# Recurrent stage: a block's gate products move behind the next block's first projection, and its convolution behind the running block's chain

## The chip, the cores and the metric

One core of one Trainium2 chip. The metric is the device time of one execution in microseconds (us); lower is better. The kernel before: 1864.37 us, median of 3 runs (1861.35 to 1865.53).

## What is computed

One layer of a hybrid decoder over 1024 tokens of width 1024: an input projection, a recurrent branch, an attention branch over selected keys, a merge, and a mixture of experts. The change touches the recurrent branch. Its reference, cut to that:

```python
xr, gr, q, ckv, qi, ki, wi, mg = jnp.split(u @ w_in[l], split_pts, axis=-1)
xc = causal_dwconv(xr, conv_w[l], conv_b[l])               # width 4
r = sigmoid(einsum('bsnc,ncd->bsnd', xc_blocks, w_a) + b_a) # 10 blocks of 128 columns
i = sigmoid(einsum('bsnc,ncd->bsnd', xc_blocks, w_x) + b_x)
log_a = -LRU_C * softplus(-lam) * r
a = exp(log_a)
inp = sqrt(-expm1(2.0 * log_a)) * (i * xc)
h = scan of h[t] = a[t] * h[t-1] + inp[t]
y_a = (gelu(gr) * h) @ w_rnn_out[l]
```

## The kernel before

The kernel runs in stages: head and index, the search for the selected keys beside the projections of queries and merge gates, the recurrent stage (`rnn`), attention, merge, experts. Channels lie on the 128 partitions and tokens along the free axis, so the recurrent branch is ten independent blocks of 128 channels by 1024 tokens. Every product is made of three matmuls of split operands (`mm3`, L137 to L139: high by high, low by high, high by low); `hilo` (L97, L98) splits a tile into a high part on ACT and a low part on DVE.

For each block b the stage does this:

- `project` of the columns of xr, then of gr: per column block, two halves of 512 tokens (`proj_tile`), 24 matmuls each, into a PSUM tile `pj` of a ring of three (`mm`, bufs 3). The weight of a column block is loaded by SP into `raw_in` (ring of 3), split on ACT into `whi_in` (L127) and on DVE or POOL into `wlo_in` (L128), each a ring of 2. `next_in` issues the load and split of the next column block before a block is used. `load_in` puts the low part on POOL for the xr columns of blocks 4 to 7 and for the first xr and gr block, and on DVE for the rest.
- `ev_x` copies xr out of PSUM (L734); with the second half it calls `conv`: an ACT instruction (L741) and three DVE instructions (L745) make `xc`, `hilo` makes `xh` and `xl`, and the two gate weights `gw` are loaded and split into `gh`, `gl`.
- `ev_g` takes the gelu of gr out of PSUM into `ge` (L793, a table load ahead of it); with the second half it calls `block`.
- `block` makes the two gate products (12 matmuls into `pg`, a ring of two PSUM tiles), their sigmoids `tr` and `ti` (L766), then the chain exp (L769), tanh (L770), sqrt (L771) on ACT and on DVE L774 to L785 with the scan L783; the result `ge` goes to `g_spill` (L786).

ACT takes a table load (ACT_TABLE_LOAD) where the next function is in another table. Each engine works through its own queue in order; that order is made at build time by the scheduler of the tile layer from the order in which the code calls, its priorities and the buffers' waits, so an edit of the calling order moves instructions on all engines. After the ten blocks three column blocks of merge gates are projected (`gates_q`, `gq`, L706), and attention begins (`pk`).

Of the kernel before, what the change touches and what calls it, by code (L numbers as in the profile page):

```python
# [19 lines left out]
P = 128  # L20
D = 1024
S = 1024
KT = D // P
ST = S // P
NB = 10
# [42 lines left out]
C_XR, C_GR, C_Q, C_KV, C_QI, C_KI, C_MG, C_END = 0, 1280, 2560, 3584, 3840, 4352, 4424, 6472  # L68
# [13 lines left out]
class Trunk:  # L82
# [638 lines left out]
    def rnn(self):  # L721
        nc, io = self.nc, self.io
        with ExitStack() as st:
            p1 = self.pool(st, "rnn")
            pp = self.pool(st, "rnnps", bufs=2, space=PSUM)
            F = lambda n, b, dt=F32, bufs=1, w=S: p1.tile([P, w], dt, name=f"{n}_{b}", tag=n, bufs=bufs)
            cur = {}

            def ev_x(c, m, ts_, ps):
                b = c // P  # L730
                if ts_.start == 0:
                    cur[b] = F("xr", b, w=S + 3, bufs=2)
                    nc.gpsimd.memset(cur[b][:, 0:3], 0.0)
                nc.scalar.activation(cur[b][:, 3 + ts_.start : 3 + ts_.stop], ps, AF.Copy)  # L734
                if ts_.stop == S:
                    cur[b] = conv(b, cur.pop(b))

            def conv(b, xr):
                c1 = slice(b, b + 1)
                xc, xh, xl = F("xc", b), F("xh", b, F32R), F("xl", b, F32R)  # L740
                nc.scalar.activation(  # L741
                    xc, xr[:, 3 : 3 + S], AF.Identity, scale=self.cw[:, 3 * NB + b : 3 * NB + b + 1], bias=self.cb[:, c1]
                )
                for w in (2, 1, 0):
                    nc.vector.scalar_tensor_tensor(  # L745
                        xc, xr[:, w : w + S], self.cw[:, w * NB + b : w * NB + b + 1], xc,
                        op0=OP.mult, op1=OP.add,
                    )
                self.hilo(xh, xl, xc)
                gh = p1.tile([P, 2, P], F32R, name=f"gh_{b}", tag="gh", bufs=2)  # L750
                gl = p1.tile([P, 2, P], F32R, name=f"gl_{b}", tag="gl", bufs=2)
                gw = p1.tile([P, 2, P], F32, name=f"gw_{b}", tag="gw", bufs=2)
                nc.sync.dma_start(gw[:, 0, :], io["w_rg_a"][0, b])
                nc.sync.dma_start(gw[:, 1, :], io["w_rg_x"][0, b])
                self.hilo(gh, gl, gw)
                return xc, xh, xl, gh, gl

            def block(b, xc, xh, xl, gh, gl):
                c1 = slice(b, b + 1)
                tr, ti = F("tr", b), F("ti", b)  # L760
                for g, (dst, bias) in enumerate(((tr, self.ba), (ti, self.bx))):
                    for h in range(2):
                        s_ = slice(h * 512, (h + 1) * 512)
                        ps = pp.tile([P, 512], F32, name=f"pg_{b}_{g}_{h}", tag="pg")
                        self.mm3(ps, gh[:, g, :], gl[:, g, :], xh[:, s_], xl[:, s_], True, True)
                        nc.scalar.activation(dst[:, s_], ps, AF.Sigmoid, bias=bias[:, c1])  # L766
                sq, w0, w1 = F("sq", b), F("w0", b), F("w1", b)

                nc.scalar.activation(w0, tr, AF.Exp, scale=self.sp8n[:, c1])  # L769
                nc.scalar.activation(tr, tr, AF.Tanh, scale=self.sp4[:, c1])  # L770
                nc.scalar.activation(sq, tr, AF.Sqrt)  # L771
                nc.vector.tensor_tensor(ti, ti, xc, op=OP.mult)

                nc.vector.tensor_scalar(w0, w0, 0.5, 0.5, op0=OP.mult, op1=OP.add)  # L774
                nc.vector.scalar_tensor_tensor(w1, tr, 1.0, w0, op0=OP.add, op1=OP.mult)
                nc.vector.scalar_tensor_tensor(w1, w1, 2.0, w0, op0=OP.subtract, op1=OP.mult)

                nc.vector.scalar_tensor_tensor(sq, sq, -2.0, w1, op0=OP.mult, op1=OP.mult)
                nc.vector.tensor_tensor(ti, ti, sq, op=OP.mult)

                nc.vector.tensor_tensor(tr, tr, w1, op=OP.mult)
                nc.vector.tensor_scalar(tr, tr, 2.0, 1.0, op0=OP.mult, op1=OP.add)
                nc.vector.tensor_tensor_scan(sq, tr, ti, 0.0, op0=OP.mult, op1=OP.add)  # L783
                ge = cur["g"]
                nc.vector.tensor_tensor(ge, ge, sq, op=OP.mult)  # L785
                nc.sync.dma_start(self.gd[b * P : (b + 1) * P, :], ge)  # L786

            def ev_g(c, m, ts_, ps):
                b = (c - C_GR) // P
                if ts_.start == 0:  # L790
                    cur["g"] = F("ge", b, bufs=2)
                ge = cur["g"]
                nc.scalar.activation(ge[:, ts_], ps, AF.Gelu_apprx_tanh)  # L793
                if ts_.stop == S:
                    block(b, *cur.pop(b))

            for b in range(NB):
                self.project(C_XR + b * P, C_XR + (b + 1) * P, ev_x)
                self.project(C_GR + b * P, C_GR + (b + 1) * P, ev_g)


    def attention(self):
# [910 lines left out]
```

## Time and profile before

| what | value |
|---|---|
| runs | 1864.37 us median, 1861.35 to 1865.53 |
| profiled execution, its own time | 1865.06 us |
| its span | 1863.3 us |
| busy: PE, DVE, ACT, POOL | 94%, 77%, 63%, 21% of the span |
| recurrent stage | 402 to 694 us of the span, with the first two of the three `gq` column blocks |

The span begins with the first and ends with the last recorded instruction; 1.8 us lie around it. PE is TensorE's matmuls, PEld its weight loads, DVE VectorE, ACT ScalarE, POOL GpSimd, SP the queue that issues the loads. In a timeline each row has the start and the duration in us, the engine, the line, the operation, out<-in with shapes, and in brackets the idle time ahead of it with what ended that.

### The profile page before, as it was taken

The numbers are of one execution on the slowest core, as the hardware profiler recorded it, in microseconds if no ns is written. First come the engines' busy times: TensorE is split into PE (matmuls) and PEld (weight loads), VectorE is DVE, ScalarE is ACT, GpSimd is POOL, SyncE is SP. The second block draws the span as 40 slices with busy tenths as digits, with TensorE's granted clock in tenths as the row PEclk, the third lists the DMA queues.
The fourth block names the chain that finished last, engine by engine and source line by source line (L and its number), as shares of the span: only waits on it lengthen the run. The fifth ranks groups of instructions, "written<-read, shape, count | busy, mean of one in ns | idle before, by whom it ended". The sixth has DMA issues, their size and how long they took to land. (4 is left out here: it accounts for less than half of the span.)

```text
span 1863.3 us, 24597 instructions
## 1 busy us (share of the span) xinstructions
PE 1759.3 (94%) x8532; PEld 1456.1 (78%) x8532; DVE 1439.9 (77%) x2393; ACT 1170.1 (63%) x1730; POOL 398.8 (21%) x249
## 2 busy tenths in 40 slices
PE   3999999997999999999999999979999999999995
PEld 2788877786777888999788877858888888788774
DVE  6688876697777766778524456569999999999998
ACT  6565677725676767888512113348888887777765
POOL 4101002210010001212000001033554544344134
PEclk9999999998999999999999999979999999999998
DMA  9213754322112212121738544369989999999994
GB/s 297 61 35 104 237 179 147 109 89 65 59 54 73 68 58 93 55 66 57 216 107 252 194 152 170 138 238 350 379 329 344 363 376 367 366 380 371 357 338 182
DMA packets 163738, 366.85 MB, mean 197 GB/s; under 512 B 17855, under 2 KB 107543, under 8 KB 139160
## 3 DMA queue, kind: packets, MB, share of 16 engines
q1 hardware_dynamic: 152112, 340.50, 51.3%
q0 software_dynamic: 10192, 19.99, 3.9%
q10 hardware_dynamic: 1304, 4.74, 0.6%
q8 instruction: 68, 1.11, 0.3%
q14 instruction: 62, 0.51, 0.1%
HBM read 326.90 MB, written 54.53 MB: 205 GB/s over the span
## 5 line engine op out<-in xcount | busy, mean ns | idle before, releaser
L1472 ACT ACTIVATE whi<-raw_w 128x1024 fp32r<-128x1024 f32 x384 | 395.6, 1057 | 107.8 <-DMA raw_w<-in_moe_w_dram 28.2
L1474 DVE TENSOR_TENSOR wlo<-raw_w,whi 128x1024 fp32r<-128x1024 f32 x382 | 447.9, 1220 | 13.1 <-ACT whi L1472 4.7
L139 PE MATMUL pj<-uhi,wlo_in 128*128 128x512 f32 (+2 forms) x784 | 302.8, 387 | 5.6 <-POOL wlo_in L128 4.2
L137 PE MATMUL pj<-uhi,whi_in 128*128 128x512 f32 (+2 forms) x784 | 304.3, 388 | 1.2 <-ACT gq L706 1.2
L138 PE MATMUL pj<-ulo,whi_in 128*128 128x512 f32 (+2 forms) x784 | 302.0, 385 | 0.0
L1543 POOL DMA_INDIRECT h_spill<-ye,idx x30 | 179.4, 5980 | 215.0 <-DVE ye L1539 202.2
L139 PEld LDWEIGHTS pj<-uhi,wlo_in 128*128 128x128 f32 (+1 forms) x784 | 146.4, 187 | 37.8 <-POOL wlo_in L128 6.4
L137 PEld LDWEIGHTS pj<-uhi,whi_in 128*128 128x128 f32 (+1 forms) x784 | 146.6, 187 | 32.1 <-ACT gq L706 2.4
L138 PEld LDWEIGHTS pj<-ulo,whi_in 128*128 128x128 f32 (+1 forms) x784 | 146.6, 187 | 29.9 <-issue 1.0
L654 ACT ACTIVATE junk_a<-B,nt 128x768 bf16<-128x768 f32 (+2 forms) x93 | 96.8, 1041 | 49.6 <-DVE nt L650 41.2
L1501 PE MATMUL pa<-whi,xh 128*128 128x512 f32 x256 | 103.3, 403 | 0.6 <-ACT xh L97 0.5
L138 PE MATMUL py<-wlo,hh 128*128 128x512 f32 x256 | 100.9, 394 | 2.7 <-DVE wlo L1474 2.7
L1501 PE MATMUL pa<-whi,xl 128*128 128x512 f32 x256 | 100.6, 393 | 0.5 <-DVE xl L98 0.5
L137 PE MATMUL py<-gh,whi_y 128*128 128x512 f32 x256 | 99.9, 395 | 1.1 <-ACT gh L97 1.1
L1501 PE MATMUL pb<-whi,xh 128*128 128x512 f32 x256 | 100.0, 391 | 0.4 <-ACTq L1618 0.4
L139 PE MATMUL py<-gh,wlo_y 128*128 128x512 f32 x256 | 100.4, 393 | 0.0
L138 PE MATMUL py<-gl,whi_y 128*128 128x512 f32 x256 | 100.2, 393 | 0.1
L139 PE MATMUL py<-whi,hl 128*128 128x512 f32 x256 | 100.0, 391 | 0.0
L137 PE MATMUL py<-whi,hh 128*128 128x512 f32 x256 | 99.8, 400 | 0.1
L1501 PE MATMUL pb<-whi,xl 128*128 128x512 f32 x256 | 99.7, 389 | 0.0
L128 POOL TENSOR_TENSOR wlo_in<-raw_in,whi_in 128x1024 fp32r<-128x1024 f32 (+1 forms) x20 | 50.3, 2515 | 230.4 <-ACT whi_in L127 230.4
L127 ACT ACTIVATE whi_y<-raw_y 128x1024 fp32r<-128x1024 f32 x16 | 17.0, 1062 | 104.5 <-PE py L138 98.6
(403 smaller groups left out, 4119.2 us busy)
## 6 DMA issues: line engine op xcount, KB each, us to landing
raw_w<-in_moe_w_dram SPq DMA_DIRECT2D x191, 1024.0 KB, 12.6
raw_in<-in_w_in_dram SPq DMA_DIRECT2D x50, 512.0 KB, 3.5
wm<-in_w_mod_dram SPq DMA_DIRECT2D x32, 512.0 KB, 4.7
sg_spill<-gq SPq DMA_DIRECT2D x16, 512.0 KB, 2.6
sg<-sg_spill SPq DMA_DIRECT2D x32, 256.0 KB, 3.2
wm<-in_w_mod_dram SPq DMA_DIRECT2D x24, 256.0 KB, 5.8
g_spill<-ge SPq DMA_DIRECT2D x10, 512.0 KB, 2.6
gr<-g_spill SPq DMA_DIRECT2D x10, 512.0 KB, 3.6
```

The lines of the kernel that those rows point to most:

```text
L127: nc.scalar.activation(hi[:, :n], raw[:, :n], AF.Copy)
L128: eng.tensor_tensor(lo[:, :n], raw[:, :n], hi[:, :n].bitcast(F32), op=OP.subtract)
L137: mm(ps, ah, bh, start=start, stop=False)
L138: mm(ps, ah, bl, start=False, stop=False)
L139: mm(ps, al, bh, start=False, stop=stop)
L654: nc.scalar.activation(junk_a[:, :n], self.B[j], AF.Sign, bias=nt[:, i : i + 1], accum_out=cnt[:, i : i + 1])
L1472: self.last_hi = nc.scalar.activation(hi, part, AF.Copy).ins
L1474: eng.tensor_tensor(lo, part, hi.bitcast(F32), op=OP.subtract)
L1501: nc.tensor.matmul(ps, a[:, kk, :], b[:, k * DE : (k + 1) * DE], start=kk == 0 and a is xh and b is hi, stop=kk == KT - 1 and b is lo,)
L1543: nc.gpsimd.indirect_dma_start(out=self.hd, out_offset=bass.IndirectOffsetOnAxis(ap=idx, axis=0), in_=ye, in_offset=None, bounds_check=S - ...
```

## The change

`conv` and `block` are no longer called from the evacuations. The loop runs once more than there are blocks: in turn b it projects xr of block b, then issues the gate products and the chain of block b-1, then the convolution of block b, then the projection of gr of block b.

```diff
@@ -732,8 +732,6 @@
                     cur[b] = F("xr", b, w=S + 3, bufs=2)
                     nc.gpsimd.memset(cur[b][:, 0:3], 0.0)
                 nc.scalar.activation(cur[b][:, 3 + ts_.start : 3 + ts_.stop], ps, AF.Copy)
-                if ts_.stop == S:
-                    cur[b] = conv(b, cur.pop(b))
 
             def conv(b, xr):
                 c1 = slice(b, b + 1)
@@ -791,12 +789,16 @@
                     cur["g"] = F("ge", b, bufs=2)
                 ge = cur["g"]
                 nc.scalar.activation(ge[:, ts_], ps, AF.Gelu_apprx_tanh)
-                if ts_.stop == S:
-                    block(b, *cur.pop(b))
-
-            for b in range(NB):
-                self.project(C_XR + b * P, C_XR + (b + 1) * P, ev_x)
-                self.project(C_GR + b * P, C_GR + (b + 1) * P, ev_g)
+
+
+            for b in range(NB + 1):
+                if b < NB:
+                    self.project(C_XR + b * P, C_XR + (b + 1) * P, ev_x)
+                if b:
+                    block(b - 1, *parts)
+                if b < NB:
+                    parts = conv(b, cur.pop(b))
+                    self.project(C_GR + b * P, C_GR + (b + 1) * P, ev_g)
```

In the rows of the built order below, `pj_512_0` is the projection of column 512 for tokens 0 to 511: columns 0 to 1279 are xr (512 is block 4, 640 block 5), 1280 to 2559 gr (1664 is block 3, 1792 block 4). `pg_3` is a gate product of block 3; a number at the end of a name is the buffer's. In the changed file the lines behind `ev_x` stand two lower (L766 is L764, L793 is L791).

PE, around the first gate products of block 3, before:

```order
L137 MATMUL pj_512_0_4111<-uhi_0_94,whi_in512_4008 128x512
L138 MATMUL pj_512_0_4111<-ulo_0_102,whi_in512_4008 128x512
L137 MATMUL pg_3_0_0_4068<-xh_3_3992,gh_3_4000 128x512
L137 MATMUL pg_3_0_1_4073<-xh_3_3992,gh_3_4000 128x512
L139 MATMUL pj_512_0_4111<-uhi_0_94,wlo_in512_4009 128x512
L137 MATMUL pj_512_0_4111<-uhi_1_95,whi_in512_4008 128x512
L138 MATMUL pj_512_0_4111<-ulo_1_103,whi_in512_4008 128x512
L138 MATMUL pg_3_0_0_4068<-xl_3_3993,gh_3_4000 128x512
```

The same place of the changed kernel:

```order
L137 MATMUL pj_1792_0_4187<-uhi_0_94,whi_in1792_4067 128x512
L138 MATMUL pj_1792_0_4187<-ulo_0_102,whi_in1792_4067 128x512
L137 MATMUL pj_1792_512_4214<-uhi_0_94,whi_in1792_4067 128x512
L138 MATMUL pj_1792_512_4214<-ulo_0_102,whi_in1792_4067 128x512
L137 MATMUL pj_640_0_4246<-uhi_0_94,whi_in640_4182 128x512
L138 MATMUL pj_640_0_4246<-ulo_0_102,whi_in640_4182 128x512
L139 MATMUL pj_640_0_4246<-uhi_0_94,wlo_in640_4183 128x512
L137 MATMUL pg_3_0_0_4128<-xh_3_3992,gh_3_4000 128x512
L137 MATMUL pg_3_0_1_4133<-xh_3_3992,gh_3_4000 128x512
L139 MATMUL pj_1792_0_4187<-uhi_0_94,wlo_in1792_4068 128x512
```

The gates of block 3 stood behind gr of block 3; they now stand behind the whole of xr of block 4, two matmuls each of both halves of gr of block 4, and three of xr of block 5, the third of which reads a low part made on POOL. Behind the last row shown follow four more matmuls of `pj_1792_0`, then the gate products that read `xl_3`.

ACT, from the tanh of block 2 to the first convolution step of block 3, before:

```order
L770 ACTIVATE tr_2_3892<-tr_2_3892,sp4_1493 128x1024
L734 ACTIVATE xr_3_3962<-pj_384_0_3937 128x512
L771 ACT_TABLE_LOAD
L771 ACTIVATE sq_2_3914<-tr_2_3892 128x1024
L127 ACTIVATE whi_in512_4008<-raw_in512_4007 128x1024
L734 ACTIVATE xr_3_3962<-pj_384_512_3965 128x512
L97 ACTIVATE gh_4_4174<-gw_4_4176 128x256
L741 ACTIVATE xc_3_3991<-xr_3_3962,cols_85 128x1024
```

The same of the changed kernel:

```order
L768 ACTIVATE tr_2_3952<-tr_2_3952,sp4_1493 128x1024
L791 ACT_TABLE_LOAD
L791 ACTIVATE ge_3_4038<-pj_1664_0_4013 128x512
L769 ACT_TABLE_LOAD
L769 ACTIVATE sq_2_3974<-tr_2_3952 128x1024
L739 ACTIVATE xc_3_3991<-xr_3_3923,cols_85 128x1024
L791 ACT_TABLE_LOAD
```

Between tanh and sqrt there is now a gelu with a table load of its own in place of a copy; the other half of that gelu needs another load behind the convolution step.

ACT, from there to the sigmoid of block 3, before:

```order
L793 ACT_TABLE_LOAD
L793 ACTIVATE ge_3_4038<-pj_1664_0_4013 128x512
L97 ACTIVATE xh_3_3992<-xc_3_3991 128x1024
L793 ACTIVATE ge_3_4038<-pj_1664_512_4040 128x512
L127 ACTIVATE whi_in1792_4106<-raw_in1792_4105 128x1024
L766 ACT_TABLE_LOAD
L766 ACTIVATE tr_3_4066<-pg_3_0_0_4068,cols_85 128x512
```

The same of the changed kernel:

```order
L791 ACTIVATE ge_3_4038<-pj_1664_512_4040 128x512
L127 ACTIVATE whi_in1792_4067<-raw_in1792_4066 128x1024
L734 ACTIVATE xr_4_4097<-pj_512_0_4072 128x512
L97 ACTIVATE gh_4_4174<-gw_4_4176 128x256
L127 ACTIVATE whi_in640_4182<-raw_in640_4181 128x1024
L734 ACTIVATE xr_4_4097<-pj_512_512_4100 128x512
L97 ACTIVATE xh_3_3992<-xc_3_3991 128x1024
L764 ACT_TABLE_LOAD
L764 ACTIVATE tr_3_4126<-pg_3_0_0_4128,cols_85 128x512
```

The gelu and the weight split that stood between `xh` and the sigmoid stand ahead of `xh` now, with the copies of xr of the next block and one weight split more; the split `whi_in640` writes the buffer that the second half of `pj_512` reads to its end.

## Rows read from the trace of the kernel before

**Rows 1.** The page, busy time by engine over the span.

```profile
PE 1759.3 (94%) x8532; PEld 1456.1 (78%) x8532; DVE 1439.9 (77%) x2393; ACT 1170.1 (63%) x1730; POOL 398.8 (21%) x249
```

**Rows 2.** Windows, block 0's gates: length, busy PE, PEld, DVE, ACT, POOL, granted clock, DMA share, GB/s.

```profile
430.00:460.00 30.00, 26.33 (x108) 21.19 (x108) 20.66 (x18) 19.96 (x22) 0.20 (x2) 0.88 0.16 51
```

**Rows 3.** Waits, 398 to 682 us: total us, times, longest us.

```profile
ACT xh L97 <- DVE xc L745: 54.0, 9, 12.4
...
PE pg L137 <- ACT xh L97: 17.6, 5, 8.8
```

**Rows 4.** Timeline of PE, the first gate matmuls of blocks 0 to 3 and their neighbours.

```profile
424.06 0.39 PE L139 MATMUL pj<-uhi,wlo_in 128*128 128x512 f32 x1
433.21 0.80 PE L137 MATMUL pg<-xh,gh 128*128 128x512 f32 x1 [8.75 <-ACT xh L97]
...
436.77 0.52 PE L137 MATMUL pj<-uhi,whi_in 128*128 128x512 f32 x1
...
460.25 0.73 PE L137 MATMUL pg<-xh,gh 128*128 128x512 f32 x2
...
485.49 0.73 PE L137 MATMUL pg<-xh,gh 128*128 128x512 f32 x2
...
487.22 0.39 PE L138 MATMUL pg<-xl,gh 128*128 128x512 f32 x1
...
512.78 0.73 PE L137 MATMUL pg<-xh,gh 128*128 128x512 f32 x2 [1.98 <-ACT xh L97]
```

**Rows 5.** Timeline of ACT, from `xh` of block 1 to `xh` of block 2.

```profile
459.13 1.06 ACT L97 ACTIVATE xh<-xc 128x1024 fp32r<-128x1024 f32 x1 [3.70 <-DVE xc L745]
...
461.64 1.28 ACT L766 ACT_TABLE_LOAD   x1
462.94 1.27 ACT L766 ACTIVATE tr<-pg,cols 128x512 f32<-128x512 f32 x2
...
470.18 0.59 ACT L734 ACTIVATE xr<-pj 128x512 f32<-128x512 f32 x1
470.79 1.28 ACT L771 ACT_TABLE_LOAD   x1
472.08 1.06 ACT L771 ACTIVATE sq<-tr 128x1024 f32<-128x1024 f32 x1
...
484.38 1.06 ACT L97 ACTIVATE xh<-xc 128x1024 fp32r<-128x1024 f32 x1 [3.70 <-DVE xc L745]
```

**Rows 6.** Timeline of DVE, blocks 0 and 2.

```profile
427.01 1.22 DVE L128 TENSOR_TENSOR wlo_in<-raw_in,whi_in 128x1024 fp32r<-128x1024 f32 x1
...
484.26 1.22 DVE L128 TENSOR_TENSOR wlo_in<-raw_in,whi_in 128x1024 fp32r<-128x1024 f32 x1
...
485.73 1.22 DVE L98 TENSOR_TENSOR xl<-xc,xh 128x1024 fp32r<-128x1024 f32 x1
```

**Rows 7.** Timelines of POOL and DVE where both work.

```profile
391.05 2.39 POOL L128 TENSOR_TENSOR wlo_in<-raw_in,whi_in 128x1024 fp32r<-128x1024 f32 x1 [8.49 <-ACT whi_in L127]
...
527.42 2.91 POOL L128 TENSOR_TENSOR wlo_in<-raw_in,whi_in 128x1024 fp32r<-128x1024 f32 x1 [15.54 <-ACT whi_in L127]
...
526.86 1.22 DVE L781 TENSOR_TENSOR tr<-tr,w 128x1024 f32<-128x1024 f32 x1
527.99 3.42 DVE L779 TENSOR_TENSOR ti<-ti,sq 128x1024 f32<-128x1024 f32 x1
```

**Rows 8.** Timelines of ACT and PE, the end of the stage.

```profile
593.53 1.06 ACT L97 ACTIVATE xh<-xc 128x1024 fp32r<-128x1024 f32 x1 [6.46 <-DVE xc L745]
...
669.57 1.04 ACT L97 ACTIVATE xh<-xc 128x1024 fp32r<-128x1024 f32 x1
...
673.29 1.27 ACT L766 ACTIVATE tr<-pg,cols 128x512 f32<-128x512 f32 x2 [0.89 <-PE pg L139]
...
672.86 0.40 PE L139 MATMUL pg<-xh,gl 128*128 128x512 f32 x1
...
693.78 0.39 PE L137 MATMUL pj<-uhi,whi_in 128*128 128x512 f32 x1
```

## The prediction

> **What bounds the kernel now.** I read the page first, then a window, the waits and the timelines of the recurrent stage. PE is busy for 94% of the span [rows 1], so over the whole kernel the order of PE's work decides, and PE's idle stretches are what a reordering can give back. In the recurrent stage the window of block 0's gates shows PE busy for 26.33 of 30 us at a mean granted clock of 0.88 [rows 2]. The waits name the cause: PE stood 17.6 us, in five stretches, for `xh`, and ACT's `xh` stood 54.0 us for DVE's `xc` [rows 3]. The longest stretch is block 0: PE ends gr at 424.06 and starts the gates at 433.21, 8.75 us idle [rows 4]; there DVE was still at the search. That is the most that the edit can fill in one place.
>
> The stage has a second limit, and the timelines show it. A block is 96 projection and 12 gate matmuls. From 424.06 back they start 0.2265 us apart (46 of them in 10.42 us), so PE alone needs 24.5 us a block. But the gates of blocks 1, 2 and 3 start at 460.25, 485.49 and 512.78 [rows 4]: 25.2 and 27.3 us apart. The reader should see in ACT's rows that this is a closed loop. From `xh` at 459.13 ACT has no gap until the sqrt ends at 473.14 (14.0 us), and from there DVE needs until `xh` at 484.38 (11.2 us) [rows 5]: chain of block b, then `xc` of block b+1, then its `xh`. 14.0 + 11.2 = 25.2, the period. The blocks with a weight split on POOL have 2.1 us more: POOL's split takes 2.39 us alone, 2.91 us where it begins behind a running DVE instruction, and DVE's next, which takes 1.22 us otherwise, then takes 3.42 [rows 7].
>
> **The change, step by step.** I walk the loop in the new order with the durations of these rows. No arithmetic is added; one table load per block is, and nine of them stand in the loop.
>
> *Block 0.* PE goes on from gr 0 into xr 1, but the third matmul of that needs a low part that DVE makes at 427.01 to 428.23 [rows 6], so about 3.5 of the 8.75 us stay idle. The other 46 matmuls take 10.4 us: 438.7. After the 8.75 us of idling the clock was at its lower level, and the six matmuls from 433.21 to 436.77 took 3.6 us for 1.4 [rows 4], part of it a wait for `xl`; after 1.98 us [rows 4] the projections kept their pace. For 3.5 us I take 0.9, under half of that loss (bounds 0 and 2.2): the gates start at 439.6. ACT first splits the weight of xr 2, whose buffer xr 1 reads to its end, copies the half of xr 1 (0.6), and loads the sigmoid table (1.29): the first sigmoid at 442.4.
>
> *From sigmoid to sqrt.* The stretch from the first sigmoid to the end of tanh stays as it is, 462.94 to 470.18, 7.24 us. Then a table load (1.29) and the gelu (0.61, the price of the copy that stood there) come ahead of the sqrt's load and the sqrt (2.35) [rows 5]: 11.5 us, 1.3 more than before. With DVE's 11.2, `xh` of block 1 starts at 442.4 + 22.7 = 465.1, 6.0 us later than at 459.13.
>
> *Block 1.* Between `xh` and sigmoid ACT has a copy, a split and a load, as now: 3.8 us [rows 5]. `xh` of block 2 starts at 465.1 + 3.8 + 22.7 = 491.6, against 484.38.
>
> *Ordinary blocks.* Copy and split have moved ahead of `xh`, so ACT could begin the sigmoid 2.3 us after `xh`. It can't, since the gate product is not there: `xl` starts 1.35 us after `xh` [rows 6], the first matmul on it 2.84 us after `xh` (487.22), and the sigmoid begins 0.43 us after the start of the next matmul (672.86 to 673.29) [rows 8]: 2.84 + 0.23 + 0.43 = 3.5 us. The period is 3.5 + 11.5 + 11.2 = 26.2 us, where it was 25.2. PE's 24.5 us lie under it.
>
> *Blocks 2 to 5* need a low part from POOL for the third of the matmuls that now stand ahead of their gates. Its split on ACT has to wait until PE has ended the projection that still reads that buffer, some 25 us after the `xh` before, so that POOL starts while DVE is at the last step of `xc`. DVE's next instruction is the low part of gr, then the small `gl`, then `xl`: they wait for POOL's 2.4 us. The gates' second matmul comes at 5.0 instead of 2.84 us after `xh`, the sigmoid at 5.7. Period 5.7 + 22.7 = 28.4, where it was 27.3. I looked for cover and found none: DVE is on the loop throughout.
>
> *Sum to block 9.* 491.6 + 4 x 28.4 = 605.2 for `xh` of block 6 (593.53 before) and + 3 x 26.2 = 683.8 for block 9 (669.57 before) [rows 8]: 14.2 us behind.
>
> *The end.* Before, PE had 101 matmuls between the gates of block 9 and the third merge column, which it began at 693.78 [rows 8]. Now the xr and gr work lies ahead, and after 34 matmuls PE stands before a projection whose PSUM buffer is freed by the first `gq`, which ACT does behind the whole chain of block 9. `xh` to sigmoid is 4.3 us there (11 matmuls between the two gate parts), then 7.24, 2.35, a load 1.29 and `gq` 0.60: 15.8 us, so PE resumes at 699.6 and after 24 matmuls (5.4) begins the third column at 705.0. That is 11.2 us behind. PE's idling of some 6 us before it may put its first matmuls at the lower clock: 0 to 2.2, I take 0.9. From that column on PE's order is unchanged and PE bound, so the delay stays.
>
> Sum: +12.1 us against the profiled 1865.06, 1877.2; that execution was 0.7 above the median of 1864.37. I forecast 1877.
>
> *The added load, weighed.* Each table load of the stage takes 1.28 us, and what follows starts at once (461.64 to 462.94) [rows 5]; 1.29 is in the sum. The Trainium skill, ScalarE: Activation LUTs, What ACT_TABLE_LOAD costs, adds a drain of about 1.38 us to every switch, 2.66 in all, and advises grouping calls by table, which speaks against this order. By it nine loads would cost 12 us more and the sum would be 1890; no row here has that gap.
>
> **Rivals.**
> - *POOL's split falls clear of the loop.* If POOL's split fell where DVE is idle, as it waits for the sigmoids, blocks 2 to 5 would go at 26.2: 8.8 us less, +3.3, some 1868, no difference that counts (0.2%, 3.7 us, is about what a measurement of this kernel can tell from no change). For it: POOL's start hangs on PE's end within half a microsecond. Against: DVE waits wherever POOL meets a two-input instruction [rows 7], and the loop leaves it no gap.
> - *The projection ahead covers the loop: faster.* If gates and chain were no longer the limit, PE would run from 439.6 through its 1032 matmuls to the third column: 439.6 + 233.7 = 673.3, 20 us sooner, 1844. It turns on the period: under 25.5 us on average the change gains, and at 24.5 it gains all of this. For it: the 8.75 us of block 0 do get filled, and PE has a whole projection between `xc` and the gates. Against: the loop runs through ACT and DVE, and it becomes longer by a load, not shorter.
> - *The clock falls in every POOL block.* PE idles there some 4 us in 7. If the lower clock follows, the end of xr moves by up to 2.2 us; ACT's split (1.05) and copy (0.6) of it now stand ahead of `xh` and have 0.3 us to spare, so up to 1.9 reach the loop. With half of that in four blocks and the upper bounds at start and end (2 x 1.3): + 6.4, some 1883. For it: block 0 [rows 2, 4]. Against: after 1.98 us in block 3 PE kept its pace.
> - *A table load costs twice its row*: 9 x 1.28, + 11.5, some 1888.
>
> **How the numbers follow.** Forecast 0.70, POOL clear 0.10, faster 0.05, clock 0.14, dear load 0.01. Faster is 0.05, same 0.10 and slower 0.85 (0.70 + 0.14 + 0.01). The range has to take in POOL's 8.8 us downwards and the clock upwards: 1867 to 1885, which leaves out the faster case, the dear load and the ends of the others.
>
> **What would show it.** Right: the 8.75 us before the gates of block 0 split into some 3.5 us of PE waiting for the low part of xr 1 and no wait at the gates; `xh` of block 1 some 6 us later; `xh` 28.4 us apart from block 2 to 6 and 26.2 after; PE waiting for POOL's low part and for `xl` in blocks 2 to 5; one long PE wait of about 6 us for the first `gq`; six table loads per block. Wrong: periods under 25.5, no PE wait at the end, or `xl` straight behind `xh` in blocks 2 to 5.

## Result, and the profile after

| | before | after |
|---|---|---|
| median of four runs each | 1864.95 us (1861.35 to 1867.93) | 1894.61 us (1890.99 to 1897.13) |
| ratio, 95% interval | | 1.0158 (1.0134 to 1.0183) |
| profiled execution, its own time | 1865.06 us | 1897.13 us |
| its span | 1863.3 us | 1895.4 us |

The change costs 29.7 us; 12.1 were forecast, and 1894.6 lies outside the range. The direction was right, the size was not. The two profiled spans differ by 32.1 us, 2.4 of which arise before the stage: gr of block 0 ends at 426.45 where it ended at 424.06 [rows 4]. (POOL's first split of the stage begins at 401.92 us before and 404.31 after; in the kernels below, whose heads are the same, between 399.87 and 406.19.) Below, 2.39 us are taken off where a time of after stands beside one of before.

The busy line of the page of after [rows 1]: PE is busy 16.0 us longer with as many matmuls, ACT 12.7 us (nine more instructions, the added table loads, are 9 x 1.28 = 11.5 of it), POOL 17.6 us with as many instructions; DVE is not.

```profile
PE 1775.3 (94%) x8532; PEld 1466.4 (77%) x8532; DVE 1430.5 (75%) x2393; ACT 1182.8 (62%) x1739; POOL 416.4 (22%) x249
```

The `xh` rows of ACT and some sigmoids (`tr`), after; the prediction walked from one `xh` to the next.

```profile
434.49 1.06 ACT L97 ACTIVATE xh<-xc 128x1024 fp32r<-128x1024 f32 x1 [12.46 <-DVE xc L743]
...
445.32 1.28 ACT L764 ACT_TABLE_LOAD   x1
446.61 1.26 ACT L764 ACTIVATE tr<-pg,cols 128x512 f32<-128x512 f32 x2
...
469.32 1.06 ACT L97 ACTIVATE xh<-xc 128x1024 fp32r<-128x1024 f32 x1 [5.33 <-DVE xc L743]
...
495.84 1.06 ACT L97 ACTIVATE xh<-xc 128x1024 fp32r<-128x1024 f32 x1
...
527.55 1.06 ACT L97 ACTIVATE xh<-xc 128x1024 fp32r<-128x1024 f32 x1 [0.41 <-DVE xc L743]
...
537.04 0.69 ACT L764 ACTIVATE tr<-pg,cols 128x512 f32<-128x512 f32 x1 [7.14 <-PE pg L139]
...
560.02 1.06 ACT L97 ACTIVATE xh<-xc 128x1024 fp32r<-128x1024 f32 x1
...
623.65 1.06 ACT L97 ACTIVATE xh<-xc 128x1024 fp32r<-128x1024 f32 x1 [0.41 <-DVE xc L743]
...
627.14 1.26 ACT L764 ACTIVATE tr<-pg,cols 128x512 f32<-128x512 f32 x2 [1.13 <-PE pg L139]
...
702.23 1.06 ACT L97 ACTIVATE xh<-xc 128x1024 fp32r<-128x1024 f32 x1 [0.74 <-DVE xc L743]
```

Set beside the walk (before's times from [rows 5, 8]), what was missed lies mostly in one place, blocks 2 to 5, and smaller parts in block 0 and at the end:

| stretch | forecast, us | measured, us |
|---|---|---|
| `xh` of block 1, against before | +6.0 | +7.8 |
| from there to `xh` of block 2 (25.25 before) | +1.2 | +1.3 |
| blocks 2 to 5, `xh` 495.84 to 623.65 (109.15 before) | +4.5 | +18.7 |
| blocks 6 to 8, to 702.23 (76.04 before) | +2.6 | +2.5 |
| `xh` of block 9 to the third merge column (24.21 before) | -2.1 | -0.5 |
| sum, of the unrounded values | +12.1 | +29.8 |

An ordinary period was forecast at 26.2 and is 26.2 (78.58 / 3). A period with a split on POOL was forecast at 28.4 and is 32.0 (127.81 / 4). 14.2 of the missing 17.6 us lie there. Block 3 shows what stands in such a period; first the timelines of POOL and DVE.

```profile
526.73 5.59 POOL L128 TENSOR_TENSOR wlo_in<-raw_in,whi_in 128x1024 fp32r<-128x1024 f32 x1 [26.09 <-ACT whi_in L127]
...
526.24 1.28 DVE L743 SCALAR_TENSOR_TENSOR xc<-xr,cols,xc 128x1024 f32<-128x1024 f32 x1
527.43 1.22 DVE L128 TENSOR_TENSOR wlo_in<-raw_in,whi_in 128x1024 fp32r<-128x1024 f32 x1
528.57 0.42 DVE L98 TENSOR_TENSOR gl<-gw,gh 128x256 fp32r<-128x256 f32 x1
528.90 1.22 DVE L98 TENSOR_TENSOR xl<-xc,xh 128x1024 fp32r<-128x1024 f32 x1
```

And PE in the same stretch, with the first gate matmul of block 6 for comparison:

```profile
526.25 0.39 PE L138 MATMUL pj<-ulo,whi_in 128*128 128x512 f32 x1
...
532.37 0.79 PE L139 MATMUL pj<-uhi,wlo_in 128*128 128x512 f32 x1 [4.45 <-POOL xr L733]
532.96 1.05 PE L137 MATMUL pg<-xh,gh 128*128 128x512 f32 x2
533.82 0.63 PE L139 MATMUL pj<-uhi,wlo_in 128*128 128x512 f32 x1
534.24 0.63 PE L137 MATMUL pj<-uhi,whi_in 128*128 128x512 f32 x1
...
624.76 0.73 PE L137 MATMUL pg<-xh,gh 128*128 128x512 f32 x2 [0.74 <-ACT xh L97]
```

I had POOL take 2.4 us and DVE wait for it. It is the other way round: DVE's low part of gr, `gl` and `xl` run at their usual lengths, `xl` 1.35 us behind `xh` as in an ordinary block, and POOL's split ends at 532.32, 2.20 us behind the end of `xl`. All four are alike: 5.24, 5.59, 5.13 and 5.56 us, each ending 4.77 us behind `xh`. PE stands before the third xr matmul meanwhile. (The row names POOL's tiny memset of `xr`, which begins as the split ends.) Then a second cost follows: matmuls start 0.43 us apart where they stood 0.2265 apart, PE's lower level. A window of 8 us from 532 (columns as in [rows 2]) shows the granted clock at 0.60; one from 718, behind the wait for the first `gq`, at 0.70.

```profile
532.00:540.00 8.00, 7.63 (x21) 6.04 (x22) 0.00 (x0) 2.76 (x4) 0.36 (x2) 0.60 0.54 150
...
718.00:726.00 8.00, 7.70 (x25) 6.15 (x26) 6.31 (x5) 1.23 (x3) 0.00 (x0) 0.70 0.10 40
```

The first sigmoid comes 4.08 us behind the first gate matmul there; in block 6, at full clock, 2.38 (624.76 to 627.14). Over the four blocks that excess is 5.7 us (1.42, 1.70, 1.63, 0.99); the other 8.5 of the 14.2 I put down to POOL's lateness; no run separates the two, since the one follows from the other. PE's waits from 400 to 722 us, all of them (total us, times, longest us):

```profile
PE pj L139 <- POOL xr L733: 17.0, 4, 4.5
PE pj L137 <- ACT gq L706: 6.9, 1, 6.9
PE pg L137 <- ACT xh L97: 4.9, 5, 2.3
PE pj L137 <- ACT xr L734: 3.7, 7, 0.6
PE pj L139 <- DVE wlo_in L128: 3.4, 1, 3.4
```

### The profile page after: what moved, and what is told of

The parts are those of the page before. It is cut to its first block, busy times and chain, and to the rows that moved or that the text cites. A ratio compares the mean times of both kernels' runs of the same rounds, so it can differ in the third digit from the quotient of the medians.

```text
span 1895.4 us, 24592 instructions
## 1 busy us (share of the span) xinstructions
PE 1775.3 (94%) x8532; PEld 1466.4 (77%) x8532; DVE 1430.5 (75%) x2393; ACT 1182.8 (62%) x1739; POOL 416.4 (22%) x249
## 5 line engine op out<-in xcount | busy, mean ns | idle before, releaser
L137 PE MATMUL pj<-uhi,whi_in 128*128 128x512 f32 (+2 forms) x784 | 308.6, 394 | 11.8 <-ACT gq L706 8.1
L1545 POOL DMA_INDIRECT h_spill<-ye,idx x30 | 186.2, 6206 | 208.6 <-DVE ye L1541 195.7
L139 PEld LDWEIGHTS pj<-uhi,wlo_in 128*128 128x128 f32 (+1 forms) x784 | 149.1, 190 | 60.6 <-POOL xr L733 18.7
L128 POOL TENSOR_TENSOR wlo_in<-raw_in,whi_in 128x1024 fp32r<-128x1024 f32 (+1 forms) x20 | 60.4, 3020 | 273.9 <-ACT whi_in L127 273.9
L127 ACT ACTIVATE whi_in<-raw_in 128x1024 fp32r<-128x1024 f32 (+1 forms) x51 | 53.4, 1046 | 73.4 <-PE pj L138 55.4
```

The costliest lines, as they stand in the source:

```text
L127: nc.scalar.activation(hi[:, :n], raw[:, :n], AF.Copy)
L128: eng.tensor_tensor(lo[:, :n], raw[:, :n], hi[:, :n].bitcast(F32), op=OP.subtract)
L137: mm(ps, ah, bh, start=start, stop=False)
L139: mm(ps, al, bh, start=False, stop=stop)
L1545: nc.gpsimd.indirect_dma_start(out=self.hd, out_offset=bass.IndirectOffsetOnAxis(ap=idx, axis=0), in_=ye, in_offset=None, bounds_check=S - ...
```

## Experiments

Times are compared by their ratio to the kernel before, which was timed again beside each group: 1867.2 us (e1 to e4), 1868.2 (v0 to v2) and 1866.7 (m1, g1).

**e1: the low parts on DVE.** The changed kernel with one condition of `load_in` taken out:

```diff
-        eng = ... or c in (C_XR, C_GR) or 4 * P <= c < 8 * P or c == C_KV + P else None
+        eng = ... or c in (C_XR, C_GR) or c == C_KV + P else None
```

> The changed kernel with the low parts of xr columns 4 to 7 made on DVE instead of POOL. Theory A (the 14 us that blocks 2 to 5 took beyond my walk are POOL's split, which DVE's string of wlo_in, gl and xl shuts out until xl is done, and the lower clock that PE's 4 us wait for it brings): the third xr matmul no longer stands ahead of the gates, xh comes 26.2 us apart in blocks 2 to 5 as in blocks 6 to 8, no PE wait over 1 us there, clock 1.00; four periods of 31.5 to 32.5 become 26.2: 23 us less, some 1871.6. Rival B (the new order itself makes these blocks long: ACT's wait for the shared weight buffer and the copies ahead of xh): the periods stay above 30 and the time above 1887. Rival C (DVE's own 1.2 us split then stands on the loop): periods 27.4, some 1876.

Measured: 1871.36 us, ratio 1.002 (1.0004 to 1.0035), some 26 us less than the change's 1.0158. Two windows of e1 (columns as in [rows 2]), PE at full clock in both:

```profile
524.00:552.00 28.00, 26.92 (x118) 21.53 (x117) 19.72 (x18) 22.06 (x24) 0.10 (x1) 1.00 0.21 65
552.00:580.00 28.00, 26.97 (x118) 21.66 (x117) 19.43 (x18) 22.08 (x26) 0.10 (x1) 1.00 0.20 61
```

Every period from block 2 on is 26.2 us. Theory A holds: what blocks 2 to 5 cost beyond an ordinary block hangs on POOL's split. Since the scheduler also put the third xr matmul elsewhere in this kernel, e1 alone does not say whether the split or its place costs.

**m1: the split stays, one matmul moves.** An order without a semaphore is set on PE, from the last gate matmul of the running block to the first matmul that reads the low part:

```diff
+            if k == 0 and ts_.start == 0 and 4 * P <= c < 8 * P:
+                self.tc.add_manual_dep(
+                    self.nc.cur_bb.bb.instructions[-1], self.last_pg,
+                    mybir.DependencyInfo(mybir.DependencyClass.NoSync, mybir.DependencyReason.DATA),
...
+                        self.last_pg = nc.cur_bb.bb.instructions[-1].name
```

> The changed kernel with POOL's splits as they are, but the third matmul of the xr projections of columns 4 to 7, the first to read POOL's low part, ordered behind the running block's gate products on PE; nothing else moves. Theory (POOL's 5.2 to 5.6 us cost only because that one matmul stands ahead of the gates on PE's queue; the lower clock follows from the wait): POOL's split is as long as before, PE does not wait for it, clock 1.00, periods 26.2 in blocks 2 to 5, four times 5.75 us less: 23 us under the changed kernel, some 1871.6, as e1. Rival (POOL also holds DVE or ACT up in those blocks): periods 28 to 30, 1878 to 1887.

Measured: 1873.35 us, ratio 1.0035 (1.002 to 1.005): e1's time. POOL's split is as slow as before and nobody waits for it; `xh` comes 26.20 us apart. POOL's timeline in m1:

```profile
519.02 5.44 POOL L128 TENSOR_TENSOR wlo_in<-raw_in,whi_in 128x1024 fp32r<-128x1024 f32 x1 [20.72 <-ACT whi_in L127]
```

So some 23 of the 29.7 us are the price of four matmuls' places on PE's queue, and the lower clock in these blocks is a consequence of the wait.

**e3: eight splits on POOL instead of four** (`2 * P <= c < 10 * P`).

> The changed kernel with the low parts of xr columns 2 to 9 on POOL, eight instead of four. Theory A: each further block whose split meets DVE's string costs the difference between a POOL block and an ordinary one, 31.95 - 26.2 = 5.8 us; of the four new ones (those of xr 2, 3, 8, 9, in blocks 0, 1, 6, 7) the first falls where DVE stands idle after block 0's xl and costs little, so three cost: 17 us more, some 1912. Rival (a POOL split costs its own 2.4 us, and the rest of the 5.8 is the start of a row of such blocks): 7 to 10 us more, 1902 to 1905.

Measured: 1906.99 us, ratio 1.0199 (1.0168 to 1.023), by the ratios 7.6 us over the change, where theory A had 17 and the rival 7 to 10. The total is the rival's; the trace is not. The periods are 31.4 to 32.5 in six blocks, not seven, and 26.5 and 26.2 in the others: the split of xr 3 came as `xl` ended, found DVE idle and took 2.39 us. Two more blocks at 5.7 us are 11.4, within what the two intervals allow, and in the traces `xh` of block 9 comes 11.3 us later than in the change, counted from POOL's first split of the stage in both. The price of a block was right, the count was not. POOL's split of xr 3 in e3:

```profile
466.55 2.39 POOL L128 TENSOR_TENSOR wlo_in<-raw_in,whi_in 128x1024 fp32r<-128x1024 f32 x1 [2.36 <-ACT whi_in L127]
```

**e4: the low part of xr 1 on POOL** (`c in (C_XR, C_GR, C_XR + P)`).

> The changed kernel with the low part of xr column 1 also on POOL, so that PE does not wait for DVE, which is at the search then. Theory: the 3.4 us PE wait at 426.9 goes and with it the lower clock behind it (2.5 us); the gates of block 0 start 5.9 us sooner and the chain of block 0 with them, though POOL's 2.4 us hold DVE's search up by as much, which xh of block 0 can bear: 5 to 6 us less, some 1889. Rival (DVE's delay moves xc, xh and xl of block 0 behind the gates' new place): 2 to 4 us less, 1890.5 to 1892.5.

Measured: 1890.86 us, ratio 1.0123 (1.0097 to 1.0148), 6.5 us under the change by the ratios, whose intervals overlap a little. In the trace PE's 3.4 us wait is gone and `xh` of block 1 comes 5.4 us sooner, counted from POOL's first split of the stage in both. That is near the 5.9 forecast (3.4 us of wait and 2.5 of clock).

**e2: the kernel before with the low parts on DVE** (e1's edit).

> The kernel before with the same low parts (xr columns 4 to 7) on DVE. Theory: DVE's L779 goes back from 3.42 to 1.22 us and the four periods from 27.3 to 25.2, but a split of 1.22 us now stands ahead of xl, 0.6 us of which shows behind xh: periods 25.2 to 25.8, 6.0 to 8.4 us less, 1856.5 to 1859. Rival: the split lands on the loop as dear as POOL's was: no change, 1863 to 1867.

Measured: 1858.52 us, ratio 0.9957 (0.9941 to 0.9972), 8 us less; the periods are 25.1 to 25.9. POOL's split cost the kernel before 2 us a block and the changed one 5.8.

**g1: the gelu in one piece, on e1.**

```diff
-                nc.scalar.activation(ge[:, ts_], ps, AF.Gelu_apprx_tanh)
+                nc.scalar.activation(ge[:, ts_], ps, AF.Copy)
...
                 nc.scalar.activation(sq, tr, AF.Sqrt)
+                ge = cur["g"]
+                nc.scalar.activation(ge, ge, AF.Gelu_apprx_tanh)
```

> e1 (low parts on DVE) with the gelu taken out of the stretch between tanh and sqrt: the halves of gr are copied out of PSUM without a table, and one gelu over the whole block follows behind the sqrt, so a block has five table loads instead of six. Theory (a load costs its row of 1.29 us and what stands between sigmoid and sqrt lies on the loop): the stretch loses 1.29 of load and keeps a 0.60 us instruction: periods 24.9 instead of 26.2, nine of them 11.7 us less than e1, a ratio of some 0.996 to the kernel before. Rival (a load costs 1.4 us more than its row): the loop falls under PE's 24.5 us and PE sets the period: 24.5, 15 us less, 0.994. Rival (the gelu behind the sqrt delays what follows on ACT, xc or xh): 25.5 or more, under 6 us less, 0.999 or more.

Measured: 1861.72 us, ratio 0.9967 (0.9955 to 0.998), 9.9 us under e1; periods of 25.1 to 25.9 where 24.9 was forecast. The theory's direction and most of its size hold, and the dear load (0.994) lies outside the interval. It is a sum of one load, a copy and what moved with them, and not the price of a load by itself.

**p1, p2, p3, p5: POOL against DVE.** Why did POOL not get its turn behind the running instruction, as in [rows 7]? Behind the ten blocks of e1 short cases were set, of this form, with the order on DVE, ACT and POOL held. `t` lets DVE start, `s` POOL; the expectations say what stands in DVE's string.

```python
nc.scalar.activation(t, src, AF.Copy)
nc.scalar.activation(s[:, 0:512], src[:, 0:512], AF.Copy)
nc.gpsimd.tensor_tensor(p, s, k, op=OP.subtract)
for o in outs:
    nc.vector.tensor_tensor(o, t, k, op=OP.subtract)
```

> A measurement, on the changed kernel with the low parts on DVE (e1), with four short cases put behind the ten blocks; its time is that of e1 and some 25 to 30 us of these cases. In each, ACT's copy lets DVE start a first two-input instruction of 1.22 us, and ACT's next copy (0.6 us) lets POOL start a 2.4 us subtraction while that runs; behind it stand three more DVE instructions. Case 0: four f32 subtractions that do not depend on each other. Case 1: four that each read the one before. Case 2: as in the changed kernel's blocks, one three-operand instruction, then three subtractions with rounded (fp32r) outputs that do not depend on each other. Case 3: as in the kernel before, the third reads the first's result, the fourth the third's. Theory A (POOL gets its turn only where DVE's next instruction waits for a result of DVE itself): POOL ends 2.2 us behind the last DVE instruction in cases 0 and 2 (5 to 6 us long), and takes 2.6 to 3.2 us in cases 1 and 3, with one DVE instruction of 3.4 us. Rival (rounded outputs or the three-operand form decide): case 0 goes like cases 1 and 3, only case 2 is long. Rival (turn by turn: POOL gets its turn behind the running instruction): all four 2.6 to 3.2 us, and the split of the changed kernel was slow for another reason.

> A second measurement of POOL against DVE, since in the first one POOL got its turn behind the running instruction in all four cases, and in the changed kernel it did not. Six cases behind the ten blocks of e1; its time is that of e1 and 50 to 60 us of these cases. Case 0 copies the place: a DVE string without gaps (two subtractions, a three-operand step of the convolution that reads its scalar from a column and its input one element off, then three subtractions with rounded outputs), POOL's subtraction with a rounded output starting near the end of the convolution step. Case 1: POOL's output is not rounded. Case 2: the three-operand step has an immediate scalar and an aligned input. Case 3: DVE's outputs are not rounded. Case 4: no convolution step, one subtraction ahead only. Case 5: two convolution steps. Theory (rounded outputs on both engines decide): POOL takes over 4.5 us in cases 0, 2, 4 and 5, under 3.3 in 1 and 3. Rival (the convolution step's form decides): over 4.5 in 0, 1, 3 and 5, under 3.3 in 2 and 4. Rival (turn by turn, always): 2.4 to 3.6 us in all six, and what shut POOL out in the changed kernel stays open.

> A third measurement of the same, five cases behind the ten blocks of e1, each with a gapless DVE string of two subtractions, a convolution step and three further subtractions, and POOL's subtraction starting in the second or third. What the changed kernel has and the first two measurements had not: its low part on DVE waits for a load and for ACT, and its gl for two loads, waits long fulfilled that stand in DVE's queue as instructions of their own. Case 0: none of these waits. Case 1: the subtraction behind the convolution step waits for ACT. Case 2: for a load and for ACT. Case 3: as case 2, and gl waits for two loads. Case 4: as case 3, and POOL also reads a loaded tile. Theory (a wait instruction between two DVE instructions lets DVE keep its turn): POOL 2.4 to 3.6 us in cases 0 and 1, over 4.5 in 3 and 4, in 2 either. Rival (turn by turn here too): 2.4 to 3.6 us in all five; then what shut POOL out stays open.

> A measurement of the same behind the ten blocks of e1, with POOL's start moved late into the convolution step (0.3 to 0.7 us before its end), as it falls in the changed kernel; in the earlier ones it fell at that step's start or into other instructions. Three independent subtractions follow it. Case 0: none of them waits for anything new. Case 1: the first waits for a load and ACT, the second for loads. Case 2: the first waits for ACT. Case 3: as case 1, with a plain subtraction in place of the convolution step. Case 4: as case 1, POOL later still. Theory (a late start loses the turn to the instruction that is already queued, and to those behind it): 4.3 to 5.2 us in cases 0, 1, 2 and 4 and perhaps 3. Rival (the waits in DVE's queue decide together with the late start): only 1, 4 and perhaps 3. Rival (turn by turn): 2.5 to 3.0 us in all; then the question stays open.

Measured: in all twenty cases POOL's split ends 2.2 us behind the DVE instruction during which it began, and DVE's next, where the string has one, takes 2.6 to 3.4 us, or 2.2 us more than alone. No theory of mine for the delay stood: neither rounded outputs, nor the convolution step, nor fulfilled waits in DVE's queue, nor a late start. The closest copy is p5's case 1; its rows of POOL and DVE:

```profile
713.62 2.68 POOL L828 TENSOR_TENSOR xh<-w,tr 128x1024 fp32r<-128x1024 f32 x1 [8.20 <-ACT w L827]
...
712.81 1.28 DVE L834 SCALAR_TENSOR_TENSOR w<-xr,cols,w 128x1024 f32<-128x1024 f32 x1
714.01 3.36 DVE L841 TENSOR_TENSOR xl<-ge,xc 128x1024 fp32r<-128x1024 f32 x1
```

**p4: the real meeting, with one thing changed in each block.**

> The kernel of e3 (low parts of xr columns 2 to 9 on POOL), with one thing of the meeting changed in each of several blocks, since 15 copies of it behind the stage all went turn by turn. The split of xr 4 stays as it was. With xr 5, the low part that DVE makes at that moment (of gr 5) lies in another pool's buffer. With xr 6, DVE has no gl of block 6 to make (ACT copies the unsplit gate weight instead). With xr 7, DVE has no low part of gr 7 to make (ACT copies the unsplit weight instead): so block 6's gates and gr 7 lose or falsify their low-by-high terms. With xr 8 the low part of xr 8 itself lies in the other buffer. With xr 9, DVE clears the first two elements of its low part first. Theory (the buffers' neighbourhood shuts POOL out): xr 4 5.2 to 5.6 us, xr 5 or xr 8 under 3.4. Rival (DVE's low part, whose waits were long fulfilled, slips in ahead of POOL and what follows keeps the turn): xr 7 under 3.4, where gl then waits for POOL, xr 4, 5 and 6 as long as their strings. Rival (POOL waits for the end of DVE's string whatever stands in it): each split ends 2.2 us behind xl: 5.2 to 5.6 us in 4 and 5, 4.8 to 5.3 in 6, 4.0 to 4.6 in 7.

Here I had the pairing wrong: the split of xr j meets DVE's low part of gr j-1, `gl` of j-1 and `xl` of j-2, so the edits fell one split later than the expectation says, and the one without `gl` met no full string. (The time, 1899.7 us in one run, tells nothing.) With the low part of gr 5 in another buffer the split still took 5.58 us, as long as without that. The split of xr 7 began one DVE instruction sooner than the others, during `ge`, and did get its turn, ahead of the last convolution step. That of xr 8 began with DVE idle and took 2.41 us. That of xr 9 began during the scan and ended 2.15 us behind it, and there it was DVE's low part that waited, 3.31 us long: that instruction does not pass POOL everywhere. POOL and DVE there (the lines of this kernel stand up to 10 lower):

```profile
589.83 2.78 POOL L137 TENSOR_TENSOR wlo_in<-raw_in,whi_in 128x1024 fp32r<-128x1024 f32 x1 [26.07 <-ACT whi_in L131]
...
589.18 1.22 DVE L797 TENSOR_TENSOR ge<-ge,sq 128x1024 f32<-128x1024 f32 x1
590.32 3.38 DVE L753 SCALAR_TENSOR_TENSOR xc<-xr,cols,xc 128x1024 f32<-128x1024 f32 x1
```

What keeps POOL out when it begins during the last convolution step of a real block, and only there, is open.

**v0, v1, v2: the convolution freed from the chain.** Of the two parts of the change, the projection ahead of the gates and the convolution behind the chain, v0 undoes the second. `block` is split behind its sigmoids, and `xc` has two buffers (the order and the second buffer were not tried apart):

```diff
                 if b:
-                    block(b - 1, *parts)
+                    gated = block(b - 1, *parts)
                 if b < NB:
                     parts = conv(b, cur.pop(b))
+                if b:
+                    chain(b - 1, *gated)
+                if b < NB:
```

v1 has e1's edit besides, v2 e1's and e4's.

> The changed kernel with one thing undone: the convolution of the next block is no longer queued behind this block's chain. The calls of a turn stand in the order projection of xr, gate products and sigmoids of the block before, convolution, chain of the block before, projection of gr; xc has two buffers. POOL keeps its splits. Theory (the loop of sigmoids, chain, convolution and gates is what the period hangs on in both kernels; PE needs 24.5 us): gates no longer wait for the chain, the periods fall to 24.5 to 25 in all blocks, POOL's split has some 13 us until PE wants it, and the end's wait for the first gq goes. PE runs from 428 to the third merge column but for the two waits of block 0: 1845 to 1852. Rival (ACT and DVE have too little time for 24.5): periods 25.5 to 26.5, 1856 to 1868. Rival (POOL's split falls on DVE's string here too): 28 in four blocks, 1862 or more.

> The same with the low parts of xr columns 4 to 7 on DVE. Theory: POOL's splits were hidden in the order of v0, so the time is v0's within 3 us: 1845 to 1852. Rival (POOL held DVE up in the loop): 6 us or more under v0.

> v1 with the low part of xr column 1 on POOL, as in e4. Theory: with PE the bound from block 0 on, its wait of 3.4 us and the lower clock behind it (2.5 us) come off in full: 5 to 6 us under v1. Rival (DVE's search, held up by POOL's 2.4 us, delays block 0's xc and so the gates): 2 to 4 us under v1.

Measured against the kernel before: v0 1854.65 us, ratio 0.9931 (0.9913 to 0.9948); v1 1854.0, 0.9919 (0.9901 to 0.9937); v2 1849.47, 0.9899 (0.9881 to 0.9916). v0 comes out 2.7 us above its range as read, while its kernel before read 3.2 us more than in the first runs. The window of v0 from the gates of block 0 to 690 us shows PE busy for 242.56 of 246 us at full clock; the gates stand 24.8 us apart, also in the blocks with a split on POOL, which took 2.40 us with DVE idle beside it. PE's wait for the first `gq`, forecast to go, is 2.50 us instead of 6.89. So the projection ahead does not lose by itself; it loses together with the convolution behind the chain, and m1 shows that most of that loss goes with four matmuls' places as well. That window and POOL's split of xr 4, in v0:

```profile
444.00:690.00 246.00, 242.56 (x1055) 196.87 (x1055) 180.05 (x161) 184.62 (x207) 10.30 (x11) 1.00 0.21 65
...
495.42 2.40 POOL L128 TENSOR_TENSOR wlo_in<-raw_in,whi_in 128x1024 fp32r<-128x1024 f32 x1 [14.89 <-ACT whi_in L127]
```

v1 can't be told from v0, as expected. v2 lies 4.5 us under v1 by medians, between theory and rival, with intervals that overlap; in the traces `xh` of block 9 comes 5.5 us sooner than in v1, counted from POOL's first split of the stage, which is the theory's 5 to 6. v2 beats both kernels of this case: 1 percent under the kernel before.

## Why the prediction was right in direction and wrong in size

- *What bounds the stage: right.* The loop of sigmoids, chain, `xc` and `xh` sets the period in both kernels. `xh` of block 1 follows the first sigmoid of block 0 by 22.71 us (446.61 to 469.32) where 22.7 was summed, and v0, which breaks the loop, runs at PE's pace.
- *Block 0: the wait right, the clock too small.* PE waited 3.4 us for the low part of xr 1 (3.5 forecast) and not at the gates. Then "under half of that loss" was the mistake: 0.9 was put down, with 2.2 as the upper bound, and 2.7 came (13.11 us from 430.67 to 443.78 for 46 matmuls that take 10.42). The same wait and the same 46 matmuls lost 1.7 us in e1 and v0 and 1.8 in m1, so the size differs from execution to execution. The matmuls behind the wait, in the profile of after, the first gate matmul with them:

```profile
426.45 0.39 PE L139 MATMUL pj<-uhi,wlo_in 128*128 128x512 f32 x1
...
430.67 0.79 PE L139 MATMUL pj<-uhi,wlo_in 128*128 128x512 f32 x1 [3.38 <-DVE wlo_in L128]
431.26 0.63 PE L137 MATMUL pj<-uhi,whi_in 128*128 128x512 f32 x1
...
443.78 0.39 PE L137 MATMUL pg<-xh,gh 128*128 128x512 f32 x1
```

  After 1.98 us of waiting before [rows 4], and after 2.29 to 2.32 in blocks 4 to 6, the pace had held; after 3.4 us it did not. I took a value between two rows of before, and nothing in them said that it lies between.
- *The table load and the gelu between tanh and sqrt: right.* Ordinary periods are 26.2, as summed with 1.29 us a load, and the first `tr` of block 0 starts at 446.61, as the load that began at 445.32 and took 1.28 ends. The Trainium skill (ScalarE: Activation LUTs, What ACT_TABLE_LOAD costs) adds 1.38 us of drain to a switch; this trace disagrees, since one such drain more in a block would have made the ordinary periods 27.6.
- *Blocks 2 to 5: the step that failed.* "They wait for POOL's 2.4 us" was read from a row in which POOL got its turn, and applied to a place where DVE had three instructions queued. POOL's split ended behind all three: a period of 32.0 us where 28.4 was summed, 8.5 us over four blocks without the clock. `xl` straight behind `xh` in these blocks was the prediction's own sign of being wrong. The Trainium skill (SBUF — State Buffer, SBUF: two separate sides) has POOL and a DVE instruction with two inputs exclude each other, whoever starts first, for the whole instruction. The twenty cases and [rows 7] agree, with 2.2 us of POOL left behind DVE's end; the meetings in the changed kernel do not fit, since there three DVE instructions ran at their usual lengths before POOL ended. The forecast's 28.4 is what exclusion in turn would give. Why the turn went otherwise stays open; that the split was late and that the place of one matmul made it dear is shown by m1.
- *The rival on the clock: right where I gave it 0.14.* "After 1.98 us in block 3 PE kept its pace" was the argument against it, but the rival itself had PE idle some 4 us in 7; it came as one wait of 4.0 to 4.5 us, and the clock fell in all four blocks, 5.7 us in sum. With the other two places (1.8 and 1.4) the clock makes some 8.9 of the 17.6 us missed, and POOL some 8.5. The two are one chain: PE waits longer, then runs slower.
- *The end: right but for the clock.* PE resumes 16.07 us behind `xh` of block 9 (15.8 forecast), and the 24 matmuls to the third merge column take 7.69 us instead of 6.3.

```profile
718.30 0.80 PE L137 MATMUL pj<-uhi,whi_in 128*128 128x512 f32 x1 [6.89 <-ACT gq L706]
...
725.99 0.39 PE L137 MATMUL pj<-uhi,whi_in 128*128 128x512 f32 x1
```

- *The faster rival* was refused for the right reason: the loop got longer. v0 shows what it needed: the convolution off the chain.

## What to carry to other kernels

Moving work of one engine ahead of a wait moves its other inputs ahead too: the projection ahead of the gates brought along one matmul whose operand came from POOL (2.39 us for what DVE makes in 1.22), and it stood in front of everything. Before filling an idle stretch ask which loop sets the period, and whether the filler lengthens it; here the same projection ahead gains 13 us with the convolution freed from the chain, and loses 30 without. Where an order adds PE waits of several us, sum it once at full clock and once with the rows at the lower one: here the clock made about half of what was missed.

## What the runs showed of the hardware that was not expected

POOL's two-input subtraction of 2.39 us took 5.1 to 5.6 us wherever it began during the last convolution step of a block (the change, e3, e4, m1, p4), ending 2.2 us behind the third DVE instruction after it, while in twenty cases made to look like this it ended 2.2 us behind the running one.

PE's pace fell to its lower level (1.2 GHz; 0.43 us between matmuls; granted clock 0.50 from 535 to 538 us of the change) behind every single wait of 3.38 us or more in this stage, in all kernels. Behind shorter ones it depended on the execution: it held behind 2.26 us in the change, 2.29 to 2.32 in the kernel before and 2.50 in v0, and fell behind 2.22 in e1, e3 and m1, 2.52 in v1 and 2.53 in v2. So a forecast can give such a wait only a range. In the change it was back at full pace 3.1 us (block 5) to 6.1 us (block 3) behind the first matmul. The same wait in v0, then in v1, with the matmul after next:

```profile
680.23 0.50 PE L137 MATMUL pj<-uhi,whi_in 128*128 128x512 f32 x1 [2.50 <-ACT gq L706]
...
680.80 0.39 PE L139 MATMUL pj<-uhi,wlo_in 128*128 128x512 f32 x1
```

```profile
678.63 0.80 PE L137 MATMUL pj<-uhi,whi_in 128*128 128x512 f32 x1 [2.52 <-ACT gq L706]
...
679.65 0.63 PE L139 MATMUL pj<-uhi,wlo_in 128*128 128x512 f32 x1
```
